# A mixture-of-experts decoder layer: order of the expert steps, a ring of eleven weight tiles, an early bias table, and gathers at the end in buffers of their own

## The chip, the cores and the metric

The kernel runs on one core of a Trainium2 chip. The metric is the device time of one execution in microseconds; several runs are taken and their median is shown. Five engines work side by side: PE multiplies matrices, DVE (vector), ACT (scalar) and POOL (GpSimd) do the rest, SP issues transfers. DMA engines move data between DRAM and on-chip memory.

## The reference, cut to what matters

A decoder layer on 512 tokens of 1024 values: layer norm, a hybrid mixer (sliding-window attention beside a spatial-gating MLP), output projection, layer norm, then a top-4-of-32 mixture of experts, whose result is added and normed.

```python
x2 = x.reshape(T, D)
logits = (x2 @ w_router + b_router).astype(jnp.float32)
top_val, top_idx = lax.top_k(logits, TOP_K)
gates = jax.nn.softmax(top_val, axis=-1).astype(x.dtype)
...
def body(acc, blk):
    tok, g, e = blk
    xb = x2[tok]
    h = clamped_swiglu(xb @ w_gate_up[e] + b_gate_up[e])
    y = (h @ w_down[e] + b_down[e]) * g[:, None]
    return acc.at[tok].add(y.astype(acc.dtype)), None
```

Each expert has w_gate_up of 1024 x 2048 and w_down of 1024 x 1024, all float32: 12.6 MB, 403 MB for the 32 experts. All of it is read once.

## The kernel before, in words

Mixer and router take the first part of the run. Then the 32 experts, sorted by how many tokens they have, are done in 21 **steps**, which the string PLAN (line 77) names in order. Step "N" is expert 0 or the last single one, computed in full float32 from the weight tiles (`raw`). "L" is one expert of up to 128 tokens whose tiles are split into a high and a low part (`split_next`: ACT casts `hi`, L281; DVE subtracts `lo`, L282) and multiplied in three products (`products`, L1463, L1464, L1466). "SS" is a pair of experts of up to 64 tokens, "XS" a wide step: an expert of up to 192 tokens and a small one; both in full float32 (L1470).

An expert's weights come in 12 **tiles** of 1 MB, 8 for the up and gate projection and 4 for down. Tiles lie in a ring of NRING_A + NRING_B + NRING_C = 3 + 5 + 2 = 10 buffers. SP issues their loads (`fetch`, L291, L299; `fetch_cols`, L307, cuts the last two down tiles of the last step by output columns) in the order of `todo`, one as each tile is taken (`take`); a load waits until its buffer is free, and what stands behind it on SP waits with it. `todo` follows `seq` (L313), the list of **phases**, which is also the order of PE's work: U (all of up), or A and B for the two column halves of a wide step, then D0 and D1 (down). For a step that isn't wide, D0 and D1 come behind the next step's U; a wide step does A, B, D0, D1 in one piece:

```python
if wide(i):
    seq += down + [(i, "A"), (i, "B"), (i, "D0"), (i, "D1")]
else:
    seq += [(i, "U")] + down
```

Every engine runs its instructions in the order in which this program issues them. `phase_up`, `phase_half` and `phase_down` issue matmuls, and between them `pump` and `turn_act` let side work go on, that is generators: `swiglu` (DVE L1524, L1527, L1528, ACT L1525), the transposes of its result into `hT` (PE L1533, ACT L1537, DVE L1539), gathers of the tokens of later steps (`xg`, `xT`, PE L1290), bias rows (`bias`, PE L1564), and the outputs. `flush` runs what is pending to its end.

The outputs of steps before LATE (19) are scaled by their gates and written by ACT's queue to `yd` in DRAM (`rows_out`, L1660, L1670). At the end `combine` brings them back: 16 indirect gathers by POOL (L1720), four for each of the four token blocks, each followed by an add to `hn` on DVE (L1712); the buffers are those named `xT` and `xg`, seven in all, so that beyond the first ones a gather waits for an add. Steps 19 and 20 are instead scattered by matmuls with a 0/1 matrix `sh` (`scatter`, L1413; `place` in `ending`, L1869, L1871), from the tile `yl`. `ending` does the last half of the last down projection (L1877), the final norm and the stores.

`residual` adds the gate-weighted down biases to `hn`: three loads of the table `b_dn` on SP (L1363), a cast on ACT (L1365), a subtraction on DVE (L1366), and matmuls (L1370) that stand among those of step 0 on PE.

Of the kernel before, what the change touches and what calls it, by code (L numbers as in the profile page):

```python
# [22 lines left out]
P = 128  # L23
# [16 lines left out]
NRING_C = 2  # L40
# [36 lines left out]
PLAN = "N SS L SS XS SS L SS L SS XS SS L SS L L SS L L SS N"  # L77
# [3 lines left out]
def kernel(ctx: ExitStack, tc: tile.TileContext, x, pos, gb_in, w_in, b_in, sinks,  # L81
# [124 lines left out]
    assert words[0] == words[-1] == "N" and nx + nl + ns == E  # L206
# [107 lines left out]
    for i in range(1, NS):  # L314
        down = [(i - 1, "D0"), (i - 1, "D1")] if i > 1 and not wide(i - 1) else []
        if wide(i):
            seq += down + [(i, "A"), (i, "B"), (i, "D0"), (i, "D1")]
        else:
            seq += [(i, "U")] + down
# [927 lines left out]
    for _ in range(10 - FETCH):  # L1247
        fetch_next()
# [155 lines left out]
    def scatter(u):  # L1404
# [185 lines left out]
    def phase_half(i, c):  # L1590

        st = state[i]
        flush()
# [3 lines left out]
        for k in range(KT):  # L1597
            if k % 2 == 0:
                ws = take(i)
            ready(i, ws, k % 2)  # L1600
            for u, a in zip(st["us"], accs):
                products(i, u, [a[:, 0], a[:, 1]], [x[:, k] for x in XT[u]], k % 2, ws, False, k == KT - 1)
            if not (c and k > 3 and turn_act(i)):
                pump(2)
        urgent.extend(swiglu(i, u, a, c) for u, a in zip(st["us"], accs))

    def phase_down(i, half):
        st = state[i]
        if half == 0:
            flush()  # L1610
# [6 lines left out]
        for k in range(half * 4, half * 4 + 4):  # L1617
            if k % 2 == 0:
                ws = take(i)
            ready(i, ws, k % 2)  # L1620
            for u, a in zip(st["us"], st["dn"]):
                b = st["dn"][1] if i == NS - 1 else a
                products(i, u, [a[:, 0], b[:, 1]], [h[:, k % 4] for h in st["hT"][u, k // 4]], k % 2, ws, k == 0, k == KT - 1)
            if not (half and k > 4 and direct(i + 1) and turn_act(i + 1)):
                if halved(i):
                    pump()
                elif k % 2:
# [405 lines left out]
```

## Time and profile before

| | |
|---|---|
| median of 3 runs | 1401.53 us (1401.17 to 1401.59) |
| the profiled execution, and its span | 1401.24 us, 1399.5 us |
| PE busy | 1248.2 us (89%), 5368 matmuls |
| DVE, ACT, POOL busy | 597.9, 408.9, 193.1 us |
| moved by DMA | 458.30 MB, mean 327 GB/s |

The span is the time from the first to the last instruction of the profiled execution; the little that is left of the time lies around it. A busy PE is not PE at its peak, and the share of busy time is a mean over stages that differ. The windows of the next but one section cut the span into stages; in a window "DMA share" is the mean busy share of the core's 16 DMA engines, and the clock is what was granted to PE.

### The profile page before, as it was taken

The page shows a single profiled execution, that of the slowest core. Times are in us where ns is not written, and L with a number is a line of the kernel's source. Part 1 is how long each engine was busy: PE and PEld are TensorE (multiplying, and loading weights), DVE is VectorE, ACT ScalarE, POOL GpSimd, SP SyncE. Part 2 cuts the span into 40 slices and gives each one's busy share as a digit, 9 for nine tenths or more (in the row PEclk, how much of TensorE's full clock was granted, in tenths as well). Part 3 has the DMA queues.
Part 4 walks back from the last instruction along what each step waited for, and adds up shares of the span by engine and source line. Part 5 has one row for each costly group of instructions (what it writes and reads, how often), then busy time and mean ns, then how long its engine had stood idle before and what let it go on. Part 6 is the DMA issues. An engine that isn't in the chain of part 4 may idle for free.

```text
span 1399.5 us, 15169 instructions
## 1 busy us (share of the span) xinstructions
PE 1248.2 (89%) x5368; PEld 685.8 (49%) x5369; DVE 597.9 (43%) x1065; ACT 408.9 (29%) x603; POOL 193.1 (14%) x266
## 2 busy tenths in 40 slices
PE   6799899678998999899898999989999999998652
PEld 4677777342735333263653533345476546745221
DVE  7657766222604010261642311043376466813356
ACT  3335442011413001141532200132165345713012
POOL 6544743000000000000000000000000000001213
PEclk9889999889999999999999999999999999999877
DMA  6210272469999996999999998899999999999931
GB/s 242 74 60 31 91 275 106 172 217 393 411 407 419 379 378 261 414 421 421 420 420 422 409 376 331 315 421 420 422 421 416 419 421 421 421 422 421 413 131 63
DMA packets 89783, 458.30 MB, mean 327 GB/s; under 512 B 10330, under 2 KB 11378, under 8 KB 44900
## 3 DMA queue, kind: packets, MB, share of 16 engines
q1 hardware_dynamic: 80356, 424.15, 75.6%
q0 software_dynamic: 5536, 20.00, 3.6%
q10 hardware_dynamic: 3808, 13.12, 2.3%
q8 instruction: 44, 0.72, 0.2%
q14 instruction: 39, 0.32, 0.1%
HBM read 441.96 MB, written 15.27 MB: 327 GB/s over the span
## 4 chain that ended last, share of the span: by engine, by line
PE 68%; DMA 15%; DVE 11%; ACT 3%; issue 2%; POOL 1%; SPq 0%; ACTq 0%; POOLq 0%; DVEq 0%
PE acc L1470 34%; DMA raw<-in_w_dn_dram 7%; PE acc L1464 6%; PE acc L1463 6%; PE acc L1466 6%; DMA raw<-in_w_gu_dram 3%; DMA xg<-yd,yrow 3%; DVE lo L282 3%; PE accA L430 2%; PE accA L432 2%; PE accA L431 2%; PE misc L1533 2%; ACT hi L281 1%; PE misc L1290 1%; PE acc L1564 1%
## 5 line engine op out<-in xcount | busy, mean ns | idle before, releaser
L1470 PE MATMUL acc<-raw,xT 128*64 128x512 f32 (+1 forms) x1664 | 446.9, 601 | 5.2 <-DMA raw<-in_w_gu_dram 5.1
L282 DVE TENSOR_TENSOR lo<-raw,hi 128x1024 fp32r<-128x1024 f32 x192 | 228.1, 1222 | 156.8 <-ACT hi L281 156.1
L1470 PEld LDWEIGHTS acc<-raw,xT 128*64 128x64 f32 (+1 forms) x1664 | 147.5, 145 | 257.8 <-issue 236.9
L281 ACT CAST hi<-raw 128x1024 fp32r<-128x1024 f32 x192 | 194.4, 1047 | 151.0 <-DMA raw<-in_w_dn_dram 67.9
L1470 PE MATMUL acc<-raw,hT 128*64 128x512 f32 (+1 forms) x816 | 210.3, 603 | 0.4 <-ACT hT L1537 0.4
L1399 POOL DMA_INDIRECT xg<-h1d,idx x22 | 22.5, 1023 | 893.9 <-DVE idx L1396 515.6
L1470 PEld LDWEIGHTS acc<-raw,hT 128*64 128x64 f32 (+1 forms) x816 | 68.7, 145 | 131.5 <-issue 126.3
L1463 PE MATMUL acc<-hi,xT 128*128 128x512 f32 x256 | 107.2, 419 | 0.0
L1464 PE MATMUL acc<-lo,xT 128*128 128x512 f32 x256 | 103.1, 403 | 0.0
L1525 ACT ACTIVATE sg<-sg 128x512 f32<-128x512 f32 x46 | 29.0, 631 | 204.8 <-DVE sg L1524 204.8
L1295 DVE TENSOR_TENSOR xT<-misc,xT 128x512 fp32r<-128x512 f32 x16 | 10.9, 690 | 179.5 <-ACT xT L1293 179.2
L1466 PE MATMUL acc<-hi,xT 128*128 128x512 f32 x256 | 81.6, 400 | 0.0
L1524 DVE TENSOR_SCALAR sg<-acc 128x512 f32<-128x512 f32 x46 | 31.5, 685 | 90.0 <-PE acc L1470 89.9
L430 PE MATMUL accA<-hi,tT 128*128 128x512 f32 x152 | 66.4, 437 | 1.3 <-ACT tT L468 1.3
L1463 PE MATMUL acc<-hi,hT 128*128 128x512 f32 x128 | 56.4, 440 | 9.3 <-ACT hi L281 9.3
L432 PE MATMUL accA<-hi,tT 128*128 128x512 f32 x152 | 62.6, 412 | 0.4 <-DVE tT L469 0.4
L1660 ACT ACTIVATE y<-acc,sl 128x512 f32<-128x512 f32 x42 | 27.1, 684 | 121.4 <-PE acc L1470 106.5
L431 PE MATMUL accA<-lo,tT 128*128 128x512 f32 x152 | 62.4, 411 | 0.0
L1464 PE MATMUL acc<-lo,hT 128*128 128x512 f32 x128 | 55.6, 434 | 6.7 <-DVE lo L282 6.7
L1463 PEld LDWEIGHTS acc<-hi,xT 128*128 128x128 f32 x256 | 49.7, 194 | 13.3 <-issue 3.1
L1533 PE MATMUL misc<-ident,sg 128*128 128x128 f32 x184 | 32.1, 302 | 26.6 <-DVE sg L1528 26.6
L1466 PEld LDWEIGHTS acc<-hi,xT 128*128 128x128 f32 x256 | 49.1, 192 | 12.2
(394 smaller groups left out, 1361.5 us busy)
## 6 DMA issues: line engine op xcount, KB each, us to landing
raw<-in_w_gu_dram SPq DMA_DIRECT2D x224, 1024.0 KB, 11.9
raw<-in_w_dn_dram SPq DMA_DIRECT2D x126, 1024.0 KB, 18.0
raw<-in_w_gu_dram SPq DMA_DIRECT2D x64, 512.0 KB, 10.8
yd<-y ACTq DMA_DIRECT2D x19, 512.0 KB, 7.7
raw<-in_w_in_dram SPq DMA_DIRECT2D x7, 1024.0 KB, 7.5
raw<-in_w_out_dram SPq DMA_DIRECT2D x4, 1024.0 KB
hn<-in_x_dram SPq DMA_DIRECT2D x4, 512.0 KB, 8.9
h1d<-hn ACTq DMA_DIRECT2D x4, 512.0 KB, 2.6
```

What stands on the lines that cost most here:

```text
L281: nc.scalar.copy(out=hi, in_=w.raw[:, 2 * h:2 * h + 2])
L282: nc.vector.tensor_sub(lo, w.raw[:, 2 * h:2 * h + 2], hi)
L430: nc.tensor.matmul(o, lhsT=a, rhs=hi, start=first, stop=False)
L431: nc.tensor.matmul(o, lhsT=a, rhs=lo, start=False, stop=False)
L432: nc.tensor.matmul(o, lhsT=b, rhs=hi, start=False, stop=last)
L1463: nc.tensor.matmul(outs[g], lhsT=lhs[0], rhs=hi[:, g], start=first, stop=False)
L1464: nc.tensor.matmul(outs[g], lhsT=lhs[0], rhs=lo[:, g], start=False, stop=False)
L1466: nc.tensor.matmul(outs[g], lhsT=lhs[1], rhs=hi[:, g], start=False, stop=last)
L1470: nc.tensor.matmul(outs[g][cs], lhsT=lhs[0][:, cs], rhs=ws[m].raw[:, 2 * q + g], start=first, stop=last)
L1524: nc.vector.tensor_scalar(g[:, 0], acc[:, 0], 7.0, None, op0=OP.min)
L1525: nc.scalar.activation(g[:, 0], g[:, 0], AF.Gelu_apprx_sigmoid)
L1533: nc.tensor.transpose(pt[:, j * P:(j + 1) * P], pick(g[:, 1], j), ident)
```

## The change

It has five parts.

- PLAN: the order of the steps differs; the last step is a pair, and the single expert that was last is now an "L" in the middle of the list. The number of experts and of weight bytes is the same.
- The ring has eleven tiles. The memory comes from the tile `yl`, which is gone; `yl`'s users take buffers named `hi` and `lo` from the pool of the split tiles.
- `seq`: the down projection of the step before a wide one stands between A and B, and the wide step's own down behind the U of the next step. In a wide step the matmuls go through two k of one unit and then two of the other.
- The bias table is loaded on ACT's queue, ahead of `residual`.
- The 16 gathers of `combine` have 16 buffers (four `xT`, two `xg`, two `y`, eight `hi`/`lo`), and the adds come behind all of them.

```diff
-NRING_C = 2
+NRING_C = 3
-PLAN = "N SS L SS XS SS L SS L SS XS SS L SS L L SS L L SS N"
+PLAN = "N SS L SS XS SS L L SS L L SS XS SS L L SS L L SS SS"
@@ seq
-        down = [(i - 1, "D0"), (i - 1, "D1")] if i > 1 and not wide(i - 1) else []
-        if wide(i):
-            seq += down + [(i, "A"), (i, "B"), (i, "D0"), (i, "D1")]
-        else:
-            seq += [(i, "U")] + down
+        down = [(i - 1, "D0"), (i - 1, "D1")] if i > 1 else []
+        seq += [(i, "A")] + down + [(i, "B")] if wide(i) else [(i, "U")] + down
@@ before residual
+    braw = mw.tile([3 * E, D], F32, name="sg")
+    for j in range(3):
+        nc.scalar.dma_start(out=braw[j * E:(j + 1) * E], in_=b_dn[0])
@@ residual
-        braw = mw.tile([3 * E, D], F32, name="sg")
-        for j in range(3):
-            nc.sync.dma_start(out=braw[j * E:(j + 1) * E], in_=b_dn[0])
-        bdn = mw.tile([3 * E, D], F32R, name="yl", bufs=1)
+        bdn = msplit.tile([P, 2, 512], F32R, name="hi").rearrange("p a b -> p (a b)")[0:3 * E]
@@ phase_half
-        for k in range(KT):
-            if k % 2 == 0:
-                ws = take(i)
-            ready(i, ws, k % 2)
+        for k in range(0, KT, 2):
+            ws = take(i)
+            ready(i, ws, 1)
             for u, a in zip(st["us"], accs):
-                products(i, u, [a[:, 0], a[:, 1]], [x[:, k] for x in XT[u]], k % 2, ws, False, k == KT - 1)
-            if not (c and k > 3 and turn_act(i)):
-                pump(2)
+                for q in range(2):
+                    products(i, u, [a[:, 0], a[:, 1]], [x[:, k + q] for x in XT[u]], q, ws, False, k + q == KT - 1)
+                if not (k > 2 * c and turn_act(i - 1 + c)):
+                    pump(2)
@@ y_tile
-        YH[u] = mw.tile([P, 2, 2, 512], F32R, name="yl", bufs=1)
+        YH[u] = [msplit.tile([P, 2, 512], F32R, name=a) for a in ("hi", "lo")]
@@ combine
-            if n % 3:
+            if n < 4:
                 g = mw.tile([P, KT, P], F32, name="xT", bufs=XTB).rearrange("p k s -> p (k s)")
+            elif n < 6:
+                g = mw.tile([P, D], F32, name="xg", bufs=AHEAD)
+            elif n < 8:
+                g = mw.tile([P, 2, 512], F32, name="y").rearrange("p c j -> p (c j)")
             else:
-                g = mw.tile([P, D], F32, name="xg", bufs=AHEAD)
+                g = msplit.tile([P, 2, 512], F32, name="hi" if n % 2 else "lo").rearrange("p c j -> p (c j)")
             nc.gpsimd.indirect_dma_start(out=g, out_offset=None, in_=yd,
                                          in_offset=bass.IndirectOffsetOnAxis(ap=yrow[:, t, j:j + 1], axis=0))
             gs.append((t, g))
             yield
-            if len(gs) > 4:
-                add()
-                yield
         while gs:
             add()
             yield
@@ the loop over seq
+            if ph in ("U", "A", "B") and before_ and before_[1] == "D1" and not wide(before_[0]):
+                flush(urgent)
+            elif ph != "D1":
+                flush()
...
             if ph == "D1":
+                if i == LATE:
+                    drain_all()
                 later.append(outputs(i))
```

In `phase_down` the loop goes by two k as well, and the places of `pump` and `flush` move with these edits. Line numbers of the changed kernel are smaller by 2 or 3 up to line 1640 and by some 10 behind it.

How this moves instructions shows in the order in which each engine has them; a row is a line of the kernel, an operation, its operands, its size and a count of equal rows. First PE around the first wide step (L1470, now L1468, with `hT` is a down projection, with `xT` an up; L1564, now L1562, are the bias rows which begin a U, A or B). Before: a single expert's down ends, the pair's down, then A without a break.

```order
L1466 MATMUL acc<-hi,hT 128x512 x2
L1470 MATMUL acc<-raw,hT 64x512 x32
L1564 MATMUL acc<-bt,sel 128x512 x4
L1470 MATMUL acc<-raw,xT 128x512 x2
L1470 MATMUL acc<-raw,xT 64x512 x4
L1290 MATMUL misc<-ident,xg 128x128 x8
L1470 MATMUL acc<-raw,xT 128x512 x2
L1470 MATMUL acc<-raw,xT 64x512 x4
L1470 MATMUL acc<-raw,xT 128x512 x2
```

Now: the end of A, the down of the pair, the bias rows of B; and further on the end of the next pair's U with the first rows of the wide step's down (128- and 64-column matmuls in turn).

```order
L1468 MATMUL acc<-raw,xT 128x512 x4
L1386 MATMUL misc<-aux,oh 128x4 x4
L1468 MATMUL acc<-raw,xT 64x512 x8
L1468 MATMUL acc<-raw,hT 64x512 x32
L1562 MATMUL acc<-bt,sel 128x512 x4
L1468 MATMUL acc<-raw,xT 128x512 x4
...
L1468 MATMUL acc<-raw,xT 64x512 x8
L1386 MATMUL misc<-aux,oh 128x8 x4
L1468 MATMUL acc<-raw,xT 64x512 x24
L1468 MATMUL acc<-raw,hT 128x512 x4
L1468 MATMUL acc<-raw,hT 64x512 x8
L1468 MATMUL acc<-raw,hT 128x512 x4
```

The pair's down moved behind A, and the wide step's own down behind the next pair's up. The second place is DVE near the end (L1712, now L1701, are the adds of the gathers; L1524, L1527, L1528, now L1522, L1525, L1526, are swiglu). Before:

```order
L1528 SCALAR_TENSOR_TENSOR sg<-sg 128x512
L282 TENSOR_TENSOR lo<-raw,hi 128x1024 x4
L1712 TENSOR_TENSOR hn<-hn,xg 128x1024
L1712 TENSOR_TENSOR hn<-hn,xT 128x1024 x2
L1712 TENSOR_TENSOR hn<-hn,xg 128x1024
...
L1712 TENSOR_TENSOR hn<-hn,xT 128x1024 x2
L1712 TENSOR_TENSOR hn<-hn,xg 128x1024
L1524 TENSOR_SCALAR sg<-acc 128x512
L1527 TENSOR_SCALAR sg<-acc 128x512
```

Now:

```order
L1525 TENSOR_SCALAR sg<-acc 128x512
L1526 SCALAR_TENSOR_TENSOR sg<-sg 128x512
L1701 TENSOR_TENSOR hn<-hn,xT 128x1024 x4
L1701 TENSOR_TENSOR hn<-hn,xg 128x1024 x2
L1701 TENSOR_TENSOR hn<-hn,y 128x1024 x2
L1701 TENSOR_TENSOR hn<-hn,lo 128x1024
L1701 TENSOR_TENSOR hn<-hn,hi 128x1024
...
L1701 TENSOR_TENSOR hn<-hn,lo 128x1024
L1701 TENSOR_TENSOR hn<-hn,hi 128x1024
L1637 SCALAR_TENSOR_TENSOR lo<-acc,sl,hi 128x512 x2
L1404 TENSOR_SCALAR sh<-itok,sl 128x512
```

The 16 adds stood ahead of the last step's swiglu and now stand behind it, ahead of the output of step 19 (L1637, scatter L1404). The third place is the bias table: before on SP, between two weight loads (L291).

```order
L1926 ISA x2
L291 ISA
L291 DMA raw<-in_w_gu_dram 128x2048
L1363 DMA sg<-in_b_dn_dram 32x1024 x3
L257 TENSOR_LOAD order
L257 ISA x2
```

Now on ACT (L1358), where L1290 are the copies of a step's tokens into `xT`, and L1363 is the cast of the table.

```order
L1054 COPY lt<-accA 64x256
L1075 DMA h1d<-hn 128x1024
L1102 ACTIVATE tk<-m_2109,tk 128x4
L1358 DMA sg<-in_b_dn_dram 32x1024
L1290 COPY xT<-accA 128x512 x2
L1358 DMA sg<-in_b_dn_dram 32x1024 x2
L1363 CAST hi<-sg 96x1024
L1290 COPY xT<-misc 128x512 x2
```

The three loads left SP's order, and on ACT one stands ahead of the two copies and two behind them.

## Rows read from the trace of the kernel before

**Rows 1.** Windows by stage: stretch, length, each engine's busy us (instructions), clock, DMA share, GB/s.

```profile
241.00:314.00 73.00, 55.18 (x154) 27.68 (x154) 19.13 (x64) 5.83 (x8) 5.21 (x9) 0.86 0.52 182
...
458.00:514.00 56.00, 56.00 (x199) 18.70 (x196) 4.41 (x10) 3.60 (x6) 1.26 (x2) 1.00 1.03 389
514.00:562.00 48.00, 47.80 (x168) 15.79 (x169) 3.87 (x6) 6.04 (x10) 0.00 (x0) 1.00 0.73 279
...
850.00:904.00 54.00, 53.80 (x198) 18.07 (x196) 3.87 (x6) 6.04 (x10) 0.00 (x0) 1.00 0.76 294
...
1053.00:1178.00 125.00, 120.94 (x554) 74.74 (x552) 77.73 (x100) 61.67 (x72) 4.94 (x7) 1.00 1.01 420
...
1300.00:1341.00 41.00, 17.75 (x65) 6.24 (x64) 17.18 (x15) 0.00 (x0) 8.52 (x9) 0.76 1.01 405
1341.00:1370.00 29.00, 25.65 (x76) 12.29 (x76) 13.51 (x21) 5.18 (x8) 2.81 (x1) 0.87 0.01 5
```

**Rows 2.** Timeline of SP, 250 to 260 us: start, length, engine, line, operation.

```profile
255.65 0.36 SPq L291 DMA_DIRECT2D raw<-in_w_gu_dram  x1
256.47 1.29 SPq L1363 DMA_DIRECT2D sg<-in_b_dn_dram  x3
```

**Rows 3.** Timeline of PE, 251 to 290 us (in brackets: idle before, releaser).

```profile
264.80 0.77 PE L1370 MATMUL misc<-yl,sh 96*128 96x512 f32 x1 [9.19 <-DVE yl L1366]
265.36 6.01 PE L1470 MATMUL acc<-raw,xT 128*128 128x512 f32 x8
...
275.56 3.60 PE L1470 MATMUL acc<-raw,xT 128*128 128x512 f32 x8
```

**Rows 4.** Timeline of ACT, 233 to 264 us.

```profile
237.43 0.59 ACT L1293 COPY xT<-accA 128x512 f32<-128x512 f32 x1 [0.31 <-PE accD L1136]
262.36 1.04 ACT L1365 CAST yl<-sg 96x1024 fp32r<-96x1024 f32 x1 [24.35 <-DMA sg<-in_b_dn_dram]
```

**Rows 5.** Timeline of PE, 440 to 560 us, the first wide step.

```profile
447.58 13.95 PE L1470 MATMUL acc<-raw,hT 128*64 128x512 f32 x64
461.47 0.73 PE L1564 MATMUL acc<-bt,sel 64*128 64x512 f32 x4
...
493.65 0.73 PE L1564 MATMUL acc<-bt,sel 64*128 64x512 f32 x4
...
557.21 0.74 PE L1564 MATMUL acc<-bt,sel 64*128 64x512 f32 x4
```

**Rows 6.** Timeline of PE, 340 to 352 us, an up behind an up.

```profile
350.35 0.80 PE L1564 MATMUL acc<-bt,sel 64*128 64x512 f32 x2 [5.38 <-DVE sg L1527]
```

**Rows 7.** Timeline of DVE, 1295 to 1345 us.

```profile
1297.38 1.22 DVE L1712 TENSOR_TENSOR hn<-hn,xg 128x1024 f32<-128x1024 f32 x1 [21.63 <-DMA xg<-yd,yrow]
1301.21 1.23 DVE L1712 TENSOR_TENSOR hn<-hn,xT 128x1024 f32<-128x1024 f32 x1 [2.61 <-DMA xT<-yd,yrow]
...
1340.98 1.23 DVE L1712 TENSOR_TENSOR hn<-hn,xg 128x1024 f32<-128x1024 f32 x1 [0.77 <-DMA xg<-yd,yrow]
1342.13 0.68 DVE L1524 TENSOR_SCALAR sg<-acc 128x512 f32<-128x512 f32 x1
```

**Rows 8.** Timeline of PE, 1278 to 1372 us.

```profile
1344.35 1.10 PE L1533 MATMUL misc<-ident,sg 128*128 128x128 f32 x4 [26.61 <-DVE sg L1528]
...
1358.05 1.49 PE L1413 MATMUL misc<-yl,sh 128*128 128x512 f32 x4
...
1364.72 4.45 PE L1877 MATMUL acc<-raw,hT 128*128 128x512 f32 x10
```

**Rows 9.** Timeline of POOL, 1285 to 1345 us.

```profile
1288.85 0.98 POOL L1720 DMA_INDIRECT xg<-yd,yrow  x1 [107.58 <-issue]
...
1298.87 0.95 POOL L1720 DMA_INDIRECT xg<-yd,yrow  x1 [2.78 <-DVE hn L1712]
```

**Rows 10.** The page's costliest groups: busy us, mean ns, idle before, releaser.

```profile
L282 DVE TENSOR_TENSOR lo<-raw,hi 128x1024 fp32r<-128x1024 f32 x192 | 228.1, 1222 | 156.8 <-ACT hi L281 156.1
...
L281 ACT CAST hi<-raw 128x1024 fp32r<-128x1024 f32 x192 | 194.4, 1047 | 151.0 <-DMA raw<-in_w_dn_dram 67.9
```

More of the change, by code (lines that the diff above doesn't have):

```diff
@@ L205 @@
     nx, nl, ns = (letters.count(c) for c in "XLS")
-    assert words[0] == words[-1] == "N" and nx + nl + ns == E
+    assert words[0] == "N" and nx + nl + ns == E
     nxt = {"X": 1, "L": 1 + nx, "S": nx + nl}
@@ L1246 @@
     turn[0] = FETCH
-    for _ in range(10 - FETCH):
+    for _ in range(NRING_A + NRING_B + NRING_C - FETCH):
         fetch_next()
@@ L1412, in scatter @@
                 for a in range(2):
-                    nc.tensor.matmul(pt, lhsT=sh[:, t * P:(t + 1) * P], rhs=y[:, a, c], start=a == 0, stop=a == 1)
+                    nc.tensor.matmul(pt, lhsT=sh[:, t * P:(t + 1) * P], rhs=y[a][:, c], start=a == 0, stop=a == 1)
                 h = hn[:, t, c * 512:(c + 1) * 512]
@@ L1576, in phase_up @@
         u = st["us"][0]
-        flush(urgent)
         accs = [ps_acc(), ps_acc()]
@@ L1608, in phase_down @@
         st = state[i]
-        if half == 0:
-            flush()
         while (half or len(st["hT"]) < len(st["us"]) or not wide(i)) and turn_act(i):
@@ L1616, in phase_down @@
                 st["dn"].append(ps_acc())
[L1617 to L1620, printed above, removed]
+        for k in range(half * 4, half * 4 + 4, 2):
+            ws = take(i)
             for u, a in zip(st["us"], st["dn"]):
[L1622 to L1627, printed above, removed]
+                for q in range(2):
+                    b = st["dn"][1] if i == NS - 1 else a
+                    ready(i, ws, q)
+                    products(i, u, [a[:, 0], b[:, 1]], [h[:, (k + q) % 4] for h in st["hT"][u, k // 4]], q, ws, k + q == 0, k + q == KT - 1)
+                    if halved(i) and not (half and k + q > 4 and i == NS - 2 and turn_act(i + 1)):
+                        pump()
+                if not halved(i) and not (half and i == NS - 2 and turn_act(i + 1)):
                     pump(2)
-    def direct(i):
-        return i < NS and (i == NS - 1 or wide(i + 1)) and not wide(i)
     scat = []
@@ L1645, in output @@
         gcol = SL[u][:, 1:2]
-        nc.scalar.activation(y[:, 0, c], a, AF.Copy, scale=gcol)
+        nc.scalar.activation(y[0][:, c], a, AF.Copy, scale=gcol)
         yield
-        nc.vector.scalar_tensor_tensor(y[:, 1, c], a, gcol, y[:, 0, c], op0=OP.mult, op1=OP.subtract)
+        nc.vector.scalar_tensor_tensor(y[1][:, c], a, gcol, y[0][:, c], op0=OP.mult, op1=OP.subtract)
     def y_tile(u):
         settle(1)
-        YH[u] = mw.tile([P, 2, 2, 512], F32R, name="yl", bufs=1)
+        YH[u] = [msplit.tile([P, 2, 512], F32R, name=a) for a in ("hi", "lo")]
         return YH[u]
@@ L1868, in place @@
             for j in range(2):
-                nc.tensor.matmul(pt, lhsT=sh[:, t * P:(t + 1) * P], rhs=y[:, j, c], start=j == 0, stop=j == 1)
+                nc.tensor.matmul(pt, lhsT=sh[:, t * P:(t + 1) * P], rhs=y[j][:, c], start=j == 0, stop=j == 1)
             h = hn[:, t, c * 512:(c + 1) * 512]
@@ L1895 @@
     with in_order():
+        before_ = None
         for i, ph in seq:
@@ L1907 @@
                 phase_down(i, int(ph == "D1"))
+            before_ = i, ph
             if i == 0:
@@ L1911 @@
                 side.append([combine_rows(), 0])
-            if ph in ("U", "B"):
+            if ph in ("U", "B") and i < NS - 1:
                 for ent in [e for e in side if e not in scat]:
```

1 line of the change is left out of this document (removed).

## The prediction

> **What bounds the kernel now.** I read the windows by stage first, then the timelines of the engines at each place where a stage loses transfer time. The windows [rows 1] split the run in three. Up to 314 us the DMA engines are half idle (share 0.52, 182 GB/s) while PE waits or works at a granted clock of 0.86. From 314 to 1341 they are full (share 1.01, about 420 GB/s), except late in the two wide steps, where the share is 0.73 (514 to 562) and 0.76 (850 to 904) and PE is busy all the time. After 1341 nothing more is loaded, and 58.5 us remain to the end of the span. So the weight stream sets the end of its long stage, and a saving counts if it starts that stream earlier, keeps it full, or shortens what stands behind it. PE is no loose second: from 1053 it is busy 121 of 125 us. A tile of 1.05 MB takes 2.5 us at 420 GB/s.
>
> **The change part by part,** against the span of 1399.5 us; the profiled execution took 1401.24 us (1.74 more), 0.3 us under the median of the runs, 1401.53.
>
> 1. *Bias table.* SP issues the table's three loads at 256.47, behind a weight load of 255.65 that had waited for a ring slot [rows 2]. ACT converts it at 262.36, idle for 24.35 us [rows 4], and PE stands 9.19 us for it at 264.80 [rows 3]. The next eight matmuls take 6.01 us where later ones take 3.60: 2.4 more. Now the loads are issued by ACT around its copies into xT (237.43, [rows 4]); from 256.47 to 262.36 load and issue took 5.9 us, so the table is there by some 245, before the 264.80 − 9.19 = 255.6 at which PE wants it. On ACT only the copies of 0.59 us stand behind the issues. Saved: 9.19 + 2.4 = **11.6**; 9.2 if the slow matmuls stay, 12.5 with the issue and its place on SP (1.29) gone too. PE frees the ring's slots in this stage, so the stream shifts by as much. The Trainium skill ("DMA: Bandwidth & Descriptors", section "Issuing engines are not separate DMA queues") says that issuing from another engine saves only the time of the issue: by that the term would be the 1.29 us of the issue. The rows differ: what was late was the issue's place behind a wait.
>
> 2. *Ring of eleven.* One more tile is loaded ahead while step 0 computes: one tile, **2.5**; nothing if PE frees slots too late to matter, so 0 to 2.5.
>
> 3. *Wide steps.* Full share would be 1.01: (1.01 − 0.73) × 48 / 1.01 = 13.3 and (1.01 − 0.76) × 54 / 1.01 = 13.4 us are lost, 26.7 in all [rows 1]. Why: the halves A and B start at 461.47 and 493.65, 32.2 us apart [rows 5], for 8 tiles that load in 8 × 1.05 MB / 389 GB/s = 21.6. With some 1.5 us of other transfers, PE falls 9 us behind in each half. The down projection takes 557.21 − 493.65 − 32.2 = 31.4 for 8 tiles of 2.5, 10 behind: 28 in a row. The share falls at about 514, 52.5 us into the block; at 9 per 32.2 plus the 1.5 that is a lag of 15 to 17 us, the ring's reserve. Now the order is A, down of the pair before, B, up of the next, down of the wide step. A pair's down takes 13.95 [rows 5] for 8 tiles (20 us): −6; a pair's up (16 tiles, 40 us) takes two times that and some 4 of small matmuls: −8. The lag runs +9, +3, +12, +4, +14, and the single expert's up behind it adds perhaps 4 (from 1053 on PE and stream are near even): 18, against a reserve of 17 plus 2.5 for the eleventh tile. It just fits, so I leave 5 us for what the new seams add: up of the next step now stands behind the swiglu of B, and a seam of this kind cost 5.38 us [rows 6]. **−21.7**, bounds 10 and 28 (all of it, and half the switches between 128- and 64-column matmuls, some 0.3 us a block). The slower rate of the wide tiles (389 GB/s) stays.
>
> 4. *The end.* The 16 adds on DVE stand ahead of the last step's swiglu: from 1297.38, each held by its gather, to 1340.98, and only then the swiglu, 1342.13 [rows 7]. POOL issues gathers from 1288.85, and waits for adds to free buffers from 1298.87 on [rows 9]. PE is idle 26.61 us until 1344.35 and does the last step's down projection when all weights lie there [rows 8]; its last weight matmul ends at 1364.72 + 4.45 = 1369.2, and 30.3 us of scatter, norm and stores follow. Now the 16 gathers have buffers of their own, POOL waits for no add, and the adds stand behind the swiglu. The last step is a pair: in its last half PE needs 16 matmuls after the last tile, at 13.95 / 64 = 0.22 [rows 5] 3.5 us, about 1 after it lands; the norm's parameters load behind that tile for 2.5. New tail: −2.5 + 1 + 3.5 + 30.3 = 32.3 against 58.5: **−26.2**. It needs the adds done in time. Let T be the end of step 18's down projection (1278 before). Gathers start at T + 10.9; all 16 took 52 us then (1288.85 to 1340.98), and 61 at the 3.8 us between the first two adds, so they land by T + 72. The stream ends at T + 63 plus 12 tiles, T + 93. Swiglu of step 20 comes when its up tiles are used, about T + 56, the adds are 16 × 1.23 = 20 us long and end with the last gather near T + 76; then step 19's output, its PSUM freed at T + 78. The last half needs it by T + 90. If late, only part of the 26 is had: bounds 5 and 28.
>
> 5. *Single instead of the first kind of step at the end.* The last full step becomes one split into high and low parts: 24 casts on ACT of 1.05 and 24 subtracts on DVE of 1.22 [rows 10], 25 and 29 us beside 30 us of stream. They are hidden as the other eight are: in the stretch from 1053, with two such steps, DVE is busy 78 of 125 us [rows 1]. **0**; bounds −5 (matmuls shorter than full f32) and +5.
>
> Sum: −11.6 − 2.5 − 21.7 − 26.2 = −62.0; span 1337.5, time **1339**. The bounds would give −24 (5 us against it in point 5 and the least of each) to −76; not all ends fall together.
>
> **Rivals.**
> - *The wide stall moves.* The up of the next step, and down of the wide step, wait for PSUM and swiglu, or the lag of 18 passes the reserve. For it: 18 against 19.5 is thin, and the seam of 5.38. Against: the seams before overlap mostly. Half of the 26.7 stays: 21.7 − 9 = 12.7 regained, **1348**, up to 1352.
> - *The gathers land last.* The stream stays full until its end; if the gathers get less of it than before, the adds pass T + 90, and the scatter of step 19 (1364.72 − 1358.05 = 6.7) and the last half (4.45, [rows 8]) stand bare where I count 2 us; with adds 4 us late that is 13 more: **1352**. For it: the stream ahead of them is now unbroken. Against: at 0.52 MB per 3.8 us they had 138 of 405 GB/s [rows 1], enough. The Trainium skill (same page, "Queues, rings and completion order") says each DMA engine takes turns between its queue rows packet by packet; the share of a third is in line with that, and sixteen issued at once would get no less.
> - *The early table and the ring do nothing:* ACT's loads are late all the same, or SP's next wait takes the place of the bias wait. Points 1 and 2 fall: **1353**. For it: ACT issues two of three loads behind copies which wait for PE. Against: those copies ran at 237.43.
> - *Slower: the splits become the bound.* Three times now two single experts follow each other. If casts and subtracts did not run beside each other, 24 × (1.05 + 1.22) = 54.5 us stand against 30 of stream, 24.5 lost per single expert; nine give 220: 1339 + 220 = **1559**. From 62 / 9 = 7 us per single expert the change loses. Against: the two in a row from 1053 kept the share at 1.01 and PE at 121 of 125 us.
>
> **How the numbers follow.** Forecast 0.62; wide stall 0.17; gathers 0.12; table and ring 0.05; splits 0.04. The range: below, the greatest gains of points 1 and 3 with the rest as taken (−7.2) plus some of points 4 and 5 make 1327; above, two rivals at once (1348 and 1352 give 1361) and a little of the unknown make **1365**. Outside lie the slow rival and the worst bounds. A measurement here tells about 0.2%, 2.8 us: all cases but the splits are faster by far more. Faster 0.95, same 0.01, slower 0.04.
>
> **What would show it.** Right: no bias wait of 9 us on PE before the first matmul on it; a DMA share of 1.0 through both wide blocks, without a slice of 0.75; one burst of 16 gathers on POOL; adds behind the last swiglu and done before the stream ends; some 32 us from the last transfer to the end, PE without the idle 26 us. Wrong: a share under 0.9 in the blocks' second halves with PE fully busy (reserve too small) or with PE waiting for DVE (seams); the last adds ending behind the last weight tile; PE idle on hi or lo tiles in the single experts; and a first stage that still lasts to 314.

## The result, and the profile after

| | before | after |
|---|---|---|
| median | 1401.38 us (4 runs, 1401.17 to 1401.59) | 1345.24 us (4 runs, 1342.80 to 1347.68) |
| ratio, 95% interval | | 0.9599, 0.9581 to 0.9618 |
| profiled execution, span | 1401.24, 1399.5 us | 1346.05, 1344.4 us |
| PE, DVE, ACT busy | 1248.2, 597.9, 408.9 us | 1235.7, 628.5, 432.1 us |
| mean DMA rate | 327 GB/s | 341 GB/s |

56 us went; 62 were forecast (1339, range 1327 to 1365). The spans differ by 55.1 us. The windows by stage, cut where the stages of the changed kernel are (columns as in [rows 1]):

```profile
285.00:302.00 17.00, 17.00 (x40) 8.21 (x40) 0.93 (x4) 1.17 (x2) 1.24 (x2) 0.83 0.60 204
302.00:345.00 43.00, 41.31 (x194) 18.39 (x193) 15.48 (x23) 13.63 (x17) 1.38 (x3) 1.00 0.99 400
...
478.00:508.00 30.00, 30.00 (x108) 11.20 (x107) 1.98 (x3) 2.64 (x5) 0.00 (x0) 1.00 0.86 328
...
540.00:569.00 29.00, 29.00 (x98) 10.13 (x100) 7.60 (x9) 6.43 (x9) 0.00 (x0) 1.00 1.01 422
...
860.00:890.00 30.00, 30.00 (x118) 10.80 (x116) 0.00 (x0) 1.27 (x2) 0.00 (x0) 1.00 0.88 318
...
1300.00:1310.00 10.00, 9.24 (x34) 3.55 (x33) 5.54 (x10) 0.69 (x1) 1.54 (x1) 1.00 0.82 309
1310.00:1344.40 34.40, 9.03 (x30) 3.50 (x30) 21.12 (x55) 9.16 (x19) 15.10 (x28) 0.67 0.17 64
```

The weight stream is full from 302 us (share 0.99), before it was from 314; it has a gap in each wide block (0.86, 0.88) and none in the wide step's own down projection (540 to 569: 1.01, where [rows 1] had 0.73); it ends near 1308 (1300 + 10 × 0.82 / 1.01). Behind it 36.3 us remain, before 58.5. So the stream ends 32.9 us earlier (35.8 forecast) and the tail is 22.2 us shorter (26.2 forecast).

**The start.** PE's timeline, and ACT's cast of the bias table:

```profile
254.94 0.68 PE L1368 MATMUL misc<-hi,sh 96*128 96x512 f32 x1
255.46 3.60 PE L1468 MATMUL acc<-raw,xT 128*128 128x512 f32 x8
...
281.26 0.98 PE L1386 MATMUL misc<-aux,oh 128*128 128x4 f32 x4 [5.73 <-DVE oh L1380]
283.66 0.99 PE L1386 MATMUL misc<-aux,oh 128*128 128x8 f32 x4 [1.42 <-DVE oh L1380]
```

```profile
240.17 1.05 ACT L1363 CAST hi<-sg 96x1024 fp32r<-96x1024 f32 x1 [2.39 <-DMA sg<-in_b_dn_dram]
```

The cast runs at 240.17 instead of 262.36 [rows 4], the first bias matmul on PE waits for nothing at 254.94 where [rows 3] had 9.19 us, and the eight matmuls behind it take 3.60 instead of 6.01. The waits of 5.73 and 1.42 us for slot tables, at the end of step 0, are now the largest on PE in this stage.

**The wide blocks.** PE's timeline through the first one; 432.06 is the start of A:

```profile
463.59 13.90 PE L1468 MATMUL acc<-raw,hT 128*64 128x512 f32 x64
477.42 0.73 PE L1562 MATMUL acc<-bt,sel 64*128 64x512 f32 x4
...
507.89 0.73 PE L1562 MATMUL acc<-bt,sel 64*128 64x512 f32 x4
...
539.87 28.93 PE L1468 MATMUL acc<-raw,hT 128*128 128x512 f32 x96
```

The order is A, the pair's down (463.59), B (477.42 to 507.89), the next pair's up, the wide step's down (539.87 to 568.7). No row waits: the 5.38 us of [rows 6] that I expected at a seam did not come. Yet the DMA engines stop in B. Here is SP's wait for loads, first of the kernel before, late in its first wide step (505 to 565 us), then of the changed kernel in B (470 to 491 us); columns: waiting line, releaser, us in total, times, longest.

```profile
SPq L291 <- PE acc L1470: 34.9, 6, 7.9
```

```profile
SPq L295 <- DMA yd<-y: 10.7, 1, 10.7
```

Before, SP waits for PE's matmuls to free ring buffers. In the changed kernel it stands 10.7 us in one piece until an output's write to DRAM has landed. ACT issues that write here, and the line of 40 slices over 430 to 500 us (1.75 us each) shows 39 and 0 GB/s in 482.5 to 486.0:

```profile
478.86 0.33 ACTq L1659 DMA_DIRECT2D yd<-y  x1
```

```profile
GB/s 389 386 386 389 400 225 174 276 393 426 431 431 417 426 435 431 412 431 401 385 405 379 384 391 386 389 387 387 390 325 39 0 198 205 323 323 372 419 440 421
```

**The end.** POOL's gathers, DVE's adds, and PE (timelines):

```profile
1226.09 0.98 POOL L1713 DMA_INDIRECT xT<-yd,yrow  x1 [106.95 <-DMA yd<-y]
...
1236.11 0.94 POOL L1713 DMA_INDIRECT lo<-yd,yrow  x1 [0.30 <-PE acc L1468]
1239.44 0.94 POOL L1713 DMA_INDIRECT hi<-yd,yrow  x1 [2.39 <-DMA xT<-yd,yrow]
...
1262.11 1.98 POOL L1713 DMA_INDIRECT hi<-yd,yrow  x1 [2.42 <-DMA raw<-in_w_dn_dram]
```

```profile
1256.79 0.69 DVE L1522 TENSOR_SCALAR sg<-acc 128x512 f32<-128x512 f32 x1 [44.35 <-PE acc L1468]
...
1260.79 5.00 DVE L1701 TENSOR_TENSOR hn<-hn,xT 128x1024 f32<-128x1024 f32 x4
...
1292.59 1.23 DVE L1701 TENSOR_TENSOR hn<-hn,hi 128x1024 f32<-128x1024 f32 x1 [2.52 <-DMA hi<-yd,yrow]
1293.73 0.74 DVE L1637 SCALAR_TENSOR_TENSOR lo<-acc,sl,hi 128x512 fp32r<-128x512 f32 x1
```

```profile
1296.21 3.65 PE L1468 MATMUL acc<-raw,hT 128*64 128x512 f32 x14 [1.33 <-DMA raw<-in_w_dn_dram]
1299.79 0.50 PE L1411 MATMUL misc<-hi,sh 128*128 128x512 f32 x1
...
1310.02 0.50 PE L1859 MATMUL misc<-hi,sh 128*128 128x512 f32 x1 [0.77 <-ACT hi L1635]
1310.44 3.65 PE L1867 MATMUL acc<-raw,hT 128*64 128x512 f32 x14
```

Nine gathers go out 1.25 us apart, 1226.09 to 1236.11; from the tenth on they come 3.8 us apart, each as the gather eight before it lands, to 1262.11. The last swiglu runs at 1256.79, the adds start behind it at 1260.79, the last one at 1292.59 (it waited 2.52 us for its gather), and step 19's output follows at 1293.73. PE waits for weight tiles up to 1296.21 and from 1299.79 to 1314.09 (1310.44 + 3.65) works without a wait for one.

### The profile page after: what moved, and what is told of

The parts are those of the page before. It is cut to its first block, busy times and chain, and to the rows that moved or that the text cites. A ratio compares the mean times of both kernels' runs of the same rounds, so it can differ in the third digit from the quotient of the medians.

```text
span 1344.4 us, 15346 instructions
## 1 busy us (share of the span) xinstructions
PE 1235.7 (92%) x5416; PEld 696.9 (52%) x5417; DVE 628.5 (47%) x1093; ACT 432.1 (32%) x627; POOL 193.6 (14%) x267
## 4 chain that ended last, share of the span: by engine, by line
PE 69%; DMA 15%; DVE 10%; ACT 3%; issue 2%; POOL 1%; SPq 0%; ACTq 0%; DVEq 0%; POOLq 0%
PE acc L1468 32%; DMA raw<-in_w_dn_dram 9%; PE acc L1462 7%; PE acc L1461 7%; PE acc L1464 7%; DMA raw<-in_w_gu_dram 4%; DVE lo L282 3%; PE accA L427 2%; PE accA L428 2%; PE accA L429 2%; PE misc L1531 2%; PE misc L1287 1%; ACT hi L281 1%; PE acc L1562 1%; PE misc L1386 1%
## 5 line engine op out<-in xcount | busy, mean ns | idle before, releaser
L1468 PE MATMUL acc<-raw,xT 128*64 128x512 f32 (+1 forms) x1600 | 411.0, 602 | 7.9 <-DMA raw<-in_w_gu_dram 7.9
L282 DVE TENSOR_TENSOR lo<-raw,hi 128x1024 fp32r<-128x1024 f32 x216 | 256.4, 1223 | 170.0 <-ACT hi L281 168.9
L281 ACT CAST hi<-raw 128x1024 fp32r<-128x1024 f32 x216 | 218.3, 1047 | 142.8 <-DMA raw<-in_w_gu_dram 67.8
L1468 PEld LDWEIGHTS acc<-raw,xT 128*64 128x64 f32 (+1 forms) x1600 | 135.4, 144 | 233.8 <-issue 212.2
L1468 PE MATMUL acc<-raw,hT 128*64 128x512 f32 (+1 forms) x768 | 200.8, 608 | 11.5 <-DMA raw<-in_w_dn_dram 11.4
L1397 POOL DMA_INDIRECT xg<-h1d,idx x22 | 22.2, 1009 | 832.5 <-DVE sg L1522 401.9
L1468 PEld LDWEIGHTS acc<-raw,hT 128*64 128x64 f32 (+1 forms) x768 | 66.4, 146 | 139.0 <-issue 118.3
L1461 PE MATMUL acc<-hi,xT 128*128 128x512 f32 x288 | 117.5, 408 | 0.0
L1462 PE MATMUL acc<-lo,xT 128*128 128x512 f32 x288 | 113.9, 396 | 0.0
L1522 DVE TENSOR_SCALAR sg<-acc 128x512 f32<-128x512 f32 x46 | 31.5, 685 | 146.6 <-PE acc L1468 146.4
L1464 PE MATMUL acc<-hi,xT 128*128 128x512 f32 x288 | 90.7, 396 | 0.0
L1461 PEld LDWEIGHTS acc<-hi,xT 128*128 128x128 f32 x288 | 54.3, 189 | 14.2 <-issue 2.8
L1464 PEld LDWEIGHTS acc<-hi,xT 128*128 128x128 f32 x288 | 54.1, 188 | 13.0
L1462 PEld LDWEIGHTS acc<-lo,xT 128*128 128x128 f32 x288 | 54.2, 188 | 11.3
L1535 ACT COPY hT<-misc 128x512 f32<-128x512 f32 x28 | 16.4, 587 | 134.8 <-PE misc L1531 134.0
```

Source lines behind the costliest of these rows:

```text
L281: nc.scalar.copy(out=hi, in_=w.raw[:, 2 * h:2 * h + 2])
L282: nc.vector.tensor_sub(lo, w.raw[:, 2 * h:2 * h + 2], hi)
L1461: nc.tensor.matmul(outs[g], lhsT=lhs[0], rhs=hi[:, g], start=first, stop=False)
L1462: nc.tensor.matmul(outs[g], lhsT=lhs[0], rhs=lo[:, g], start=False, stop=False)
L1464: nc.tensor.matmul(outs[g], lhsT=lhs[1], rhs=hi[:, g], start=False, stop=last)
L1468: nc.tensor.matmul(outs[g][cs], lhsT=lhs[0][:, cs], rhs=ws[m].raw[:, 2 * q + g], start=first, stop=last)
```

## The experiments

Each is the changed kernel with the edit shown, unless said otherwise; times are medians of five runs (twelve in experiment 5), with the ratio to the kernel before; the changed kernel itself stands at 1345.24 us. The executions part by up to 5 us ahead of the experts (last section), and four or five runs of each kernel don't even that out. So where it matters the text also gives a second difference: that of the profiled executions, one of each kernel, counted from PE's first matmul of step 0 to the end of the span.

**1. The bias table back on SP.**

```diff
-    braw = mw.tile([3 * E, D], F32, name="sg")
-    for j in range(3):
-        nc.scalar.dma_start(out=braw[j * E:(j + 1) * E], in_=b_dn[0])
     def residual():
+        braw = mw.tile([3 * E, D], F32, name="sg")
+        for j in range(3):
+            nc.sync.dma_start(out=braw[j * E:(j + 1) * E], in_=b_dn[0])
```

> The changed kernel with the three loads of the bias table back on SP inside residual, all else as changed. Theory: the table is late by its place behind a weight load that waits for a ring slot; PE waits some 9 us for it again and works 2.4 us longer at the lower clock, and the whole weight stream shifts: 1345.2 + 11.6 = 1357 us (1354 to 1358). Rival: the stream is what sets the end, and the ring absorbs a wait at its start, or the issue alone is what was saved: 1346 to 1348 us.

Measured 1357.20 us (0.9682, 0.9668 to 0.9695): 12.0 us more, 11.6 forecast. PE's row has the wait of before again:

```profile
266.73 0.77 PE L1367 MATMUL misc<-hi,sh 96*128 96x512 f32 x1 [9.30 <-DVE hi L1363]
```

The saving came from the place of three small loads in a queue, and the stream carried it to the end; counted from step 0 the profiled execution is 9.2 us longer than the changed kernel's, so 12.0 is good to some 3 us.

**2. A ring of ten.** `NRING_C = 2`.

> The changed kernel with a ring of ten tiles again. Theory: the eleventh tile is one load more ahead at the start, 2.5 us, and the wide blocks' reserve is smaller by 2.5 us in each of two blocks, so 2.5 to 7.5 us slower: 1348 to 1353. Rival: the stream in the blocks is held by something other than the number of tiles, and only the start counts: 1345 to 1348.

Measured 1349.29 us (0.9631, 0.9618 to 0.9644), 4.0 us more by medians, but the five runs reach from 1344.29 to 1350.06, and the profiled one is the fastest. In that one SP's wait for the write in B is shorter than in the changed kernel's:

```profile
SPq L295 <- DMA yd<-y: 7.4, 1, 7.4
```

Counted from step 0 this execution is 1.2 us shorter than the changed kernel's. So a gain from the eleventh tile isn't shown: the medians differ by 4.0 us, within a spread of that size, and where the other four lost time stays open.

**3. The wide steps in one piece.** `seq` as before.

```diff
-        down = [(i - 1, "D0"), (i - 1, "D1")] if i > 1 else []
-        seq += [(i, "A")] + down + [(i, "B")] if wide(i) else [(i, "U")] + down
+        down = [(i - 1, "D0"), (i - 1, "D1")] if i > 1 and not wide(i - 1) else []
+        if wide(i):
+            seq += down + [(i, "A"), (i, "B"), (i, "D0"), (i, "D1")]
+        else:
+            seq += [(i, "U")] + down
```

> The changed kernel with the wide steps in one piece again (down of the pair, A, B, and the wide step's own down in a row), the two-by-two order of the units kept. Theory: the share of the DMA engines falls to about 0.75 late in both blocks as before; the changed kernel regained 26.7 - 8.4 = 18.3 us there, less 2 to 5 for the eleventh tile: 1345.2 + 13 to 18 = 1358 to 1363. Rival: most of the gain there comes from the eleventh tile or the order of the units, and the phases' order gives little: under 1352.

Measured 1359.88 us (0.9707, 0.9693 to 0.9720): 14.6 us more. Windows late in its two blocks, and SP's wait there (505 to 570 us):

```profile
508.00:540.00 32.00, 31.80 (x114) 11.40 (x110) 2.27 (x4) 2.97 (x5) 0.00 (x0) 1.00 0.79 308
...
930.00:960.00 30.00, 30.00 (x136) 10.66 (x134) 3.13 (x14) 3.60 (x6) 1.26 (x2) 1.00 0.88 343
```

```profile
SPq L291 <- PE acc L1471: 43.1, 10, 7.5
```

The share is down late in the wide steps, and SP waits for PE again as it did before (for a write only 5.9 us in the same stretch). That PE's lag beyond the ring's reserve made the loss of before, and that the order of the phases took it away, is shown by this together with experiment 5, where the loss of before stays without those writes in SP's way.

**4. The writes of the outputs on POOL.**

```diff
-            nc.scalar.dma_start(out=yd[row:row + m], in_=y[p:p + m].rearrange("p c j -> p (c j)"))
+            nc.gpsimd.dma_start(out=yd[row:row + m], in_=y[p:p + m].rearrange("p c j -> p (c j)"))
```

> The changed kernel with the writes of the outputs to DRAM issued by POOL in place of ACT. In the changed kernel the DMA engines stand nearly still from 480 to 484 us while SP waits 10.7 us, from 473.8 to 484.8, by the trace for the landing of an output's write that ACT issued at 478.9; its counterpart stands at 872. Theory: each load waits on a completion counter that it shares with the eighth transfer before it, whichever of SP and ACT issued that; a write that comes late holds the loads. With POOL the writes use other counters: the share in B of both wide blocks is 1.0, 8 us less: 1345.2 - 8 = 1337 (1335 to 1340). Rival: the ring is full there because PE is behind; the wait for the write is a coincidence: 1344 to 1347, share in B still 0.86.

Measured 1335.11 us (0.9528, 0.9515 to 0.9541): 10.1 us less than the changed kernel (11.7 counted from step 0). The windows of B's gaps in both blocks (shares of 0.63 and 0.76 in the changed kernel):

```profile
478.00:490.00 12.00, 12.00 (x43) 4.28 (x40) 0.00 (x0) 1.27 (x2) 0.89 (x2) 1.00 1.06 397
...
872.00:890.00 18.00, 18.00 (x68) 7.02 (x65) 0.00 (x0) 1.05 (x2) 0.00 (x0) 1.00 1.02 418
```

No gap is left, with PE as busy as before. So the lag did fit into the ring, and what held the loads was the write. The two gaps in B make 8.3 us (worked out in the next section); a third stands in A of the first block, where SP waits 7.4 us for the write that ACT issues at 433.46. First the changed kernel, then this one:

```profile
436.00:442.00 6.00, 6.00 (x25) 2.32 (x25) 0.00 (x0) 0.59 (x1) 0.00 (x0) 1.00 0.75 285
```

```profile
436.00:442.00 6.00, 6.00 (x23) 2.01 (x21) 0.00 (x0) 0.00 (x0) 1.01 (x3) 1.00 1.05 396
```

That is (1.05 − 0.75) × 6 / 1.05 = 1.7 us, and with the 8.3 it nearly makes the 10.1.

How write and loads hang together shows in the changed kernel's program: SP's loads of B's tiles with their waits, cut in the middle (each row is half a wide tile; the counter named is the one that the load waits for and then counts on itself):

```
L295 DMA raw<-in_w_gu_dram 128x2x512 [waits DMAHW2_49]
L295 DMA raw<-in_w_gu_dram 128x2x512 [waits DMAHW3_49,PE_49]
L295 DMA raw<-in_w_gu_dram 128x2x512 [waits DMAHW5_49]
L295 DMA raw<-in_w_gu_dram 128x2x512 [waits DMAHW6_49,PE_49]
...
L295 DMA raw<-in_w_gu_dram 128x2x512 [waits DMAHW3_49]
L295 DMA raw<-in_w_gu_dram 128x2x512 [waits DMAHW4_49,PE_49]
```

Eight completion counters, DMAHW0 to 7, go round over the transfers of SP and ACT together, in the order in which the program issues them, and a transfer waits until the one that had its counter before has landed. Between the second and the third row number 4 is missing: an output's write on ACT has it. The last row, the 13th of B's 16 halves, needs it again. A wide tile takes two counters, so the round is over after four tiles; SP runs up to eleven ahead of PE, while ACT can write only when PE has finished the down projection of the pair. With that projection between A and B, the write comes at the start of B. POOL's transfers go round eight other counters in the program, DMASW0 to 7, so SP no longer meets the writes there.

**5. The same edit on the kernel before.**

> The kernel before with one edit, the writes of the outputs to DRAM issued by POOL in place of ACT. Theory: before, the share falls to 0.75 in the wide steps because PE is some 28 us behind in a row, more than the ring holds (16 to 17 us); the late writes cost little beside it, so this gains at most 3 us: 1398 to 1402. Rival: the waits of SP for a write, not PE's lag, make most of the 26.7 us, and the new order of the phases only moved the writes: 1375 to 1390.

Measured 1402.50 us (1.0013, 1.0003 to 1.0022): no gain, as the theory says.

```profile
514.00:562.00 48.00, 47.80 (x174) 15.92 (x172) 3.87 (x6) 5.45 (x9) 1.95 (x4) 1.00 0.70 267
...
850.00:904.00 54.00, 53.80 (x198) 17.82 (x198) 3.88 (x6) 5.78 (x10) 1.94 (x4) 1.00 0.74 288
```

The shares are near those of [rows 1] (0.73, 0.76). Before, SP waits for PE in this stretch (34.9 us above) and for a write only 1.2 us, so PE's lag stands in front of the write's wait; in the new order the write's wait is what is left.

**6. The adds ahead of the last swiglu,** the 16 buffers kept.

```diff
-            if ph in ("U", "B") and i < NS - 1:
+            if ph in ("U", "B"):
```

> The changed kernel with the 16 adds ahead of the last step's swiglu on DVE, the 16 buffers kept. In the changed kernel the last gather is added at 1292.6 to 1293.8, while that swiglu runs at 1256.8. Theory: swiglu waits for the last gather, about 1294 to 1298, and the last step's down projection (14 us of PE work behind it, and its own scatter) then starts some 8 us later than the 1288.3 it had, part of it at the lower clock after an idle PE: 1345.2 + 7 to 12 = 1352 to 1357. Rival: the place of the adds is free, since PE is behind the weight tiles in any case: 1344 to 1347.

Measured 1355.00 us (0.9669, 0.9648 to 0.9691): 9.8 us more. PE waits for swiglu behind the last add, and starts again at the lower clock (granted 0.50 from 1290 to 1300 us, which is 1.2 GHz; 1.10 us for four transposes that take 0.74 otherwise):

```profile
1296.59 1.10 PE L1531 MATMUL misc<-ident,sg 128*128 128x128 f32 x4 [12.77 <-DVE sg L1526]
```

**7. Seven buffers in turn,** the loop of before in `combine`, the adds free to stand behind swiglu.

```diff
         for n in range(4 * T):
             t, j = divmod(n, 4)
-            if n < 4:
+            if n % 3:
                 g = mw.tile([P, KT, P], F32, name="xT", bufs=XTB).rearrange("p k s -> p (k s)")
...
             gs.append((t, g))
             yield
+            if len(gs) > 4:
+                add()
+                yield
```

> The changed kernel with the loop of before in combine: seven buffers in turn, and an add once five gathers are outstanding (so the first 11 adds stand ahead of the last swiglu, too). In the changed kernel POOL issues nine gathers at once and then one every 3.8 us, each as the gather eight before it lands. Theory: eight in flight or seven in flight is the same, the gathers land at the same pace (66 us from the first issue to the last add), so this costs as much as the place of the adds does, the last gathers not being ahead of swiglu: the same as that run or some 4 us less, 1349 to 1357. Rival: own buffers are what makes the gathers land in time, and with seven they are some 10 us later on top of it: over 1362.

Measured 1346.33 us (0.9611, 0.9590 to 0.9632): the same as the changed kernel. I had put the first 11 adds ahead of swiglu; only two came there. POOL does wait for adds, 18.23 us until swiglu is past, and the last add comes 3.5 us later than in the changed kernel:

```profile
1258.67 1.33 POOL L1709 DMA_INDIRECT xT<-yd,yrow  x1 [18.23 <-ACT sg L1523]
```

```profile
1296.14 1.22 DVE L1701 TENSOR_TENSOR hn<-hn,xg 128x1024 f32<-128x1024 f32 x1 [1.77 <-DMA xg<-yd,yrow]
```

Yet PE's last weight matmul ends at 1314.35 against 1314.09: PE waits only 0.60 us, at 1300.07, for what stands behind the last add. While POOL stood, the six gathers issued before were still landing, and DVE adds them from 1261.10 on without a wait. With the adds behind swiglu, buffers of their own bought nothing that these runs can tell.

**8. A single full step last,** the list ending `L L SS L SS SS N`.

> The changed kernel with a single full step at the end as before (the list ends ... L L SS L SS SS N, so one single expert goes from the middle to the end). Theory: the stream behind step 18's end is 12 tiles shorter (30 us), the gathers still need about 66 us from there beside 20 tiles, so the last add falls some 10 to 15 us behind the last weight tile in place of 12 ahead of it, and the scatter and the last half stand bare: 1345.2 + 10 to 20 = 1355 to 1365. Rival: the kind of the last step matters by its matmuls alone (PE's last half is 16 records of 0.22 us for a pair and 10 of 0.44 for a single): 1344 to 1348.

Measured 1353.12 us (0.9657, 0.9639 to 0.9676): 7.9 us more, less than the 10 to 20 expected, since the gathers speed up at the end of the weight stream: the last six adds (1292.42 to 1302.52) stand 2.0 us apart, where 3.8 was counted. PE stands for the scatter behind the last add:

```profile
1306.46 0.76 PE L1411 MATMUL misc<-hi,sh 128*128 128x512 f32 x1 [10.01 <-DVE sh L1404]
```

**9. The whole end as before:** single step last, adds ahead of its swiglu, seven buffers.

> The changed kernel with the whole end as before: a single full step last, the adds ahead of its swiglu, seven buffers in turn. Singly the first cost 7.9 us, the second 9.8 and the third 1.1. Theory: the parts lean on each other (the adds are late in either case, and a longer last step hides them only if they stand behind swiglu), and together they give the 22 us by which the tail behind the last transfer became shorter: 1345.2 + 22 = 1367 (1364 to 1371). Rival: the parts just add up or cover each other: 1364 (sum 18.8) or below 1358.

Measured 1363.83 us (0.9734, 0.9721 to 0.9747): 18.6 us more. The three singly make 9.8 + 1.1 + 7.9 = 18.8: by the medians they add up, and I expected more from their interplay. Counted from step 0 they make 7.3 + 0.0 + 7.9 = 15.2 against 19.7, so whether they lean on each other stays open. All undone parts together (12.0, 4.0, 14.6, 18.6) make 49.2 of the 56.1 us; counted from step 0, 9.2 − 1.2 + 13.0 + 19.7 = 40.7 of 54.9. Where the rest lies wasn't tried.

**10. The split adds, with the writes on POOL:** 12 adds ahead of step 19's output, the rest behind (`adds(left)` adds until `left` gathers remain), and more side work between the matmuls of the last D0.

```diff
-        while gs:
-            add()
-            yield
+        yield from adds(4)
...
             side.append(scat[-1])
+        if i == LATE:
+            side.append([adds(0), 0])
...
-                    pump(2)
+                    pump(8 if i == NS - 1 else 2)
```

> The changed kernel with POOL issuing the writes, and the end rearranged: 12 of the 16 adds ahead of step 19's output, the rest behind it, and step 19's scatter among the first half of the last step's down projection, where PE waits for tiles. In the changed kernel PE works without a wait from 1299.8 to 1314.1, 6.4 us of it step 19's scatter, while the last tile lands near 1305. Theory: PE is the bound there and the scatter can stand earlier: 2 to 4 us less than with POOL's writes alone (1335.1): 1331 to 1333. Rival: the last gathers, or the PSUM of the scatter, hold PE earlier instead: 1335 or slower.

Measured 1334.57 us (0.9522, 0.9502 to 0.9543): 0.5 us less than with the writes on POOL alone, no difference. PE:

```profile
1293.99 4.50 PE L1871 MATMUL acc<-raw,hT 128*64 128x512 f32 x18
...
1299.68 0.50 PE L1863 MATMUL misc<-lo,sh 128*128 128x512 f32 x1 [0.68 <-DVE lo L1637]
...
1300.58 3.65 PE L1871 MATMUL acc<-raw,hT 128*64 128x512 f32 x14
```

The scatter is out of the last half's way, but the adds that were put off now stand on DVE ahead of step 20's output (L1637), and PE waits between the two column halves (the row with 0.68, and 1300.58 after 1293.99 + 4.50). The work moved; it didn't go.

**11. The slot tables behind the start of step 0's down projection,** with the writes on POOL.

```diff
-            if ph in ("U", "B") and i < NS - 1:
+            if ph in ("U", "B") and 0 < i < NS - 1 or (i, ph) == (0, "D0"):
```

> The changed kernel with the writes on POOL, and in step 0 the slot tables of the next steps behind the start of its down projection instead of ahead of it. In the changed kernel PE waits 5.73 and 1.42 us for them at 281.3 and 283.7, and the transposes of swiglu and the down projection stand behind; in that stage the DMA engines are half idle. Theory: the down projection starts some 5 us earlier and the stream with it: 1335.1 - 5 = 1330 (1329 to 1332). Rival: the next step's gathers come later by the same, or the ring is what the stream waits for: 1334 to 1337.

Measured 1334.00 us (0.9521, 0.9508 to 0.9535): 1.1 us less than with the writes on POOL alone, within the spread. PE's down projection starts at 281.29, in the changed kernel at 286.99:

```profile
278.32 0.74 PE L1531 MATMUL misc<-ident,sg 128*128 128x128 f32 x4 [3.39 <-DVE sg L1526]
...
281.29 6.14 PE L1468 MATMUL acc<-raw,hT 128*128 128x512 f32 x8
...
292.76 1.01 PE L1386 MATMUL misc<-aux,oh 128*128 128x8 f32 x4 [1.33 <-DVE oh L1380]
...
302.16 0.73 PE L1562 MATMUL acc<-bt,sel 64*128 64x512 f32 x4
```

But its first eight matmuls take 6.14 us instead of 3.60 after the idle 3.39 (granted clock 0.61 from 281 to 288 us), the tables are waited for in its midst (1.33), and it ends at 302.16, where the changed kernel's ended at 302.75.

**12. All three together.**

> The changed kernel with three edits together: the writes on POOL, the slot tables of step 0 behind the start of its down projection, and the split adds with the earlier scatter at the end. The first gave 10.1 us by itself, the other two 1.1 and 0.5 us on top of it, each within its spread. Theory: one acts before the full stream and one behind it, so they add up: 1333 to 1334 (1331 to 1335). Rival: neither is real, and this is the time with the writes on POOL alone: 1335 to 1336.

Measured 1333.36 us (0.9523, 0.9498 to 0.9548), the fastest of all by its median, but not told from the writes on POOL alone (1334.12 to 1337.65 there, 1332.83 to 1336.43 here). The version to keep is the changed kernel with that one edit.

## Why the prediction was right, point by point

The direction, the four places and the order of size held. Taken on the spans, 55.1 of 62.0 us came: 6.9 too few, 3.3 of it in point 3 and 4.0 in point 4. The start is only what is left of the 32.9 us when point 3's 18.4 are taken off, 0.4 more than forecast; it takes in all else that changed in the stream, the third gap of experiment 4 too. That the sum is this near is in part luck, since undoing the parts doesn't make the whole (experiment 9). One bound in the prediction is added up wrongly: the least of each point, with 5 us against it in point 5, gives −19 and not −24.

1. *Bias table, −11.6.* Measured 12.0 by undoing it (9.2 counted from step 0), with the wait of 9.30 us on PE. What was late was the issue's place behind a wait. The section of the Trainium skill that I had weighed against it ("DMA: Bandwidth & Descriptors", "Issuing engines are not separate DMA queues") says that initiating on several engines saves only the sequencer's time for it. The 1.29 us of that reading are refuted by both figures.
2. *Ring, −2.5, bounds 0 to 2.5.* Not settled: 4.0 by medians, −1.2 counted from step 0.
3. *Wide steps, −21.7.* The gaps that are left make (1.01 − 0.86) × 30 / 1.01 + (1.01 − 0.88) × 30 / 1.01 = 8.3 us, so 18.4 of 26.7 were regained. The share under 0.9 in B with PE fully busy is the sign that I had put down for a reserve that is too small, and that reading of it was wrong: with the write's wait gone there is no gap, so the lag stays inside the reserve, as counted. No run measures the lag itself. **The step that failed is the 5 us left for "what the new seams add"**: the seams added nothing on PE; what took 8 us was the wait of SP's loads for the output write of the moved down projection, which I did not follow. I had counted each moved matmul, but not the DMA at the end of the moved phase, and not who waits for it.
4. *The end, −26.2.* The timetable from T (1216.1) held closely: first gather T + 10.0 (10.9), last add done T + 77.7 (76), stream's end T + 92 (93); only swiglu came earlier, T + 41 (56). The burst of 16 gathers didn't come; nine went out at once. So the gathers were in time, and yet the tail was 36.3 and not 32.3. **The step that failed is "16 matmuls after the last tile"**: step 19's scatter stands among the last half's matmuls, PE works on both from 1299.79 on, and ends at 1314.09, some 4 us after the 1310 of my count (stream's end 1308.1, less 2.5 for the norm's parameters, plus 1 + 3.5); the 30.3 us behind it are as counted. I had priced the scatter only in the rival in which the gathers are late. That these 4 us can be had isn't shown: moving the scatter away gave nothing (experiment 10).
5. *The splits, 0.* DVE and ACT are 31 and 23 us busier, and PE waits 6.5 and 4.0 us in all for `hi` and `lo` from 300 us on; the single experts in a row hold a share of 1.00 to 1.01. The slow rival has nothing behind it (the list has four pairs of single experts in a row, and not the three that it names).

Of the rivals, a moved wide stall came true in part, by another mechanism than the two that it names (waits for PSUM and swiglu, a lag past the reserve). That each gather gets its share beside the weights held. The gain from buffers of their own, which I had as one means of the end's gain, did not; what gave it is the place of the adds behind swiglu (9.8) and the pair as last step (7.9).

## What to carry to other kernels

A transfer's price is also its place: behind what it is issued, and which later transfer has to wait until it has landed. When a phase is moved, follow its last write as closely as its matmuls, and look at what the load queue waits for by name, since a full ring and a late write look alike in the DMA share. Sixteen buffers in place of seven bought nothing here, since little waited for the gathers that started later.

## What the runs showed that I had not expected

- Late writes of 512 KB held a weight stream of some 390 to 420 GB/s (in the first block two slices of 1.75 us near zero, less than full around them) and cost 10 us over two blocks, though they went by another engine's queue, because eight completion counters are shared. POOL's transfers have a round of eight of their own: from the tenth gather on each is issued as the one eight before it lands, 3.8 us apart beside the weights.
- The changed kernel's four runs spread over 4.9 us. The 0.4 us of the four runs before are luck: beside the experiments the kernel before reached from 1396.61 to 1405.22 us. In the profiled executions a part of this arises ahead of the experts. PE's first matmul of step 0 starts at 241.25 us in the changed kernel's and at 244.45 in that of experiment 4. Both are alike up to 163.7 us, behind the same idle 2.15 us of PE; from there to 170.5 the same matmuls take 0.39 us at a granted clock of 1.00 (2.4 GHz) in the first, and 0.63 at 0.51 (1.2 GHz) in the second. Why the clock differs there isn't shown.
